# Mixers: transition products as alternating lines, and B's transition matrices copied without the identity

## The chip, the cores and the metric

The kernel runs on one core of a Trainium2 chip: one TensorE (PE), one VectorE (DVE), one ScalarE (ACT), one GpSimd (POOL), and SyncE (SP), which issues most of the DMAs. The metric is the device time of one execution in microseconds (us), and the time of a kernel is the median of its runs. A profiled execution lists every instruction with its start and length; its lines are called "rows" below.

## The reference

The reference is one decoder block on 16 meta tokens and 1024 tokens of width 1024: a gated FFN, a mixer, a second FFN, all with RMS norms. The mixer has two branches, which share one input projection: A, a chunked gated DeltaNet with 8 heads of 128, and B, an RWKV-7 time mixing with 16 heads of 64. The change is about branch B, whose core is a recurrence over the tokens:

```python
def _rwkv7_scan(r, w, k, v, a_vec, b_vec):
    def step(state, inp):
        r_t, w_t, k_t, v_t, a_t, b_t = inp
        sa = jnp.einsum('bhvk,bhk->bhv', state, a_t)
        state = state * w_t[:, :, None, :] + sa[..., None] * b_t[:, :, None, :] \
            + v_t[..., None] * k_t[:, :, None, :]
        return state, jnp.einsum('bhvk,bhk->bhv', state, r_t)
    ...
```

Over a chunk of 64 tokens this becomes one linear step for the state S of a head: S' = gam * (S + M S) + gam * N, where M (64 x 64, the chunk's *transition* without its identity) and N (the chunk's *value part*) hold no state and can be made ahead, and gam is the decay of the chunk.

## The kernel before

The kernel has three stages: the first FFN, the mixers (`middle`), the second FFN. Only the mixers matter here. The tokens are taken in two segments of 512 (the first with the 16 meta tokens, 528 columns), and each segment in 8 steps of 128 channels: one head of A and two heads of B. So there are 16 iterations, 0 to 7 and 8 to 15. An iteration projects its inputs (the `pp` products of line 314, against weights `w` that line 162 on ScalarE and line 163 on VectorE split into two parts), prepares operands, inverts triangular blocks, builds the transitions and runs the two chains. The actions are written in the order of the string `REGULAR`, and work of neighbouring iterations is written together. A scheduler then puts the instructions of all engines in one order by its own estimate of when each can run; each engine executes its own list strictly in that order. `issue_after` ties an instruction behind another on its engine.

The places that the change touches:

- `operands` makes, among much else, `grb` and `gra` (score products, emptied by VectorE into `LT`, `UA` and `attn`), `bkt` and `vp` (transposes, emptied by ScalarE), and at line 1636 16 products `vp<-LT,Vs`.
- `transitions` (line 1808) solves two sets of products `xp` (emptied by ScalarE into `xa` and into `xv`, which lies in the tile `at`), then makes 32 products `mp` and 32 products `np`. Half of mp is M, half goes to the read-out (`AR`); half of np is N (`vbk`), half goes to the output (`yb`).
- These are 64 x 64 products: each uses one quarter of the PE array, given by the half of the partitions that it reads (`src`) and the half that it writes (`dst`). `run` (line 1333) puts products with `src == dst` and with `src != dst` into two different PSUM banks, and chunk after chunk the products change between the two kinds. Without `line` the scheduler may take one bank's products first; with `line=()` `in_line` chains them in the order written, and with a list it also makes the first product wait for the instructions of that list.
- The pool `ch` has two PSUM banks, which xp, mp, np and all products of the chains take in turn; the next user of a bank waits until its last one has been read.
- Before, VectorE reads mp: four adds of 64 x 256 elements put M plus the identity into `g.mt` (line 1839), two adds go to `AR` (line 1842).
- `chains`: `chunk_a` runs the four steps of A (products `p`, `pq`), and behind two of its products it issues `chunk_b`, one step of B: a product `b` of `g.mt` with the state, then one VectorE instruction that gives the next state `SBs[:, i + 1]` (line 1915). `bm` and `am` are the start of the chains from the meta tokens, in the first segment only. At the end come the products `bq`.

Of the kernel before, what the change touches and what calls it, by code (L numbers as in the profile page):

```python
# [26 lines left out]
CB = 64  # L27
# [1295 lines left out]
def place(i, h):  # L1323

    return (i - h) % NCB // 2
# [7 lines left out]
def run(g, pool, name, *kinds, banks=(), line=None):  # L1333


    ps, out, used, todo = dict(enumerate(banks)), [], [0, 0], []
    for f in kinds:
        ds = [f(i, 0)[2] ^ f(i, 0)[3] for i in range(2)]
        one = ds[0] == ds[1]
        at = []  # L1340
        for d in ds:
            if d not in ps:
                ps[d] = pool.tile([P, 512], F32, name=name, tag=pool.name)
            at.append(used[d])
            used[d] += NCB // 2 * CB
        for i in range(NCB):
            e, c0 = ds[i & 1], at[0] + i * CB if one else at[i & 1] + i // 2 * CB
            for h in range(2):
                l, r, src, dst = f(i, h)
                assert src ^ dst == e  # L1350
                todo.append((ps[e][HS[dst], c0 : c0 + CB], l, r))
        if one:
            out.append([(ch3(ps[ds[0]][:, at[0] : at[0] + FULL], CB), slice(0, NCB))])
        else:
            out.append([(ch3(ps[d][:, c0 : c0 + NCB // 2 * CB], CB), cs) for d, c0, cs in zip(ds, at, EO)])
    products = [lambda x=x: g.nc.tensor.matmul(x[0], lhsT=x[1], rhs=x[2], start=True, stop=True) for x in todo]  # L1356
    if line is None:
        for p in products:
            p()
    else:  # L1360
        in_line(g, products, line)
    return out
# [171 lines left out]
def operands(g, q):  # L1534
# [98 lines left out]
        k = key(i, h)  # L1633
        return Vs[HS[k], i], LT[HS[k], i, 1 - (i & 1), CB:], k, h

    for ps, cs in run(g, g.mx, "vp", vr, banks=banks)[0]:
        nc.scalar.activation(ch3(yb, CB)[:, cs], ps, AF.Copy)
    if meta:
        btm = q.btm = st.tile([64, P], F32, name="btm", tag="btm", bufs=2)
# [168 lines left out]
def transitions(g, q):  # L1808

    nc, st = g.nc, g.st  # L1810
    Y = g.Y[q.it % 2]
    AR, LT, BKt, Vs, yb = q.AR, q.LT, q.BKt, q.Vs, ch3(q.yb, CB)
    vbk = q.vbk
    xa, xv, ar = st.tile([P, NCB, CB], F32, name="xa", tag="xa"), q.at, AR[:, NCB + 1 :]
    turned_bk, va, vb = by_key(g, q)
    vka = q.vka

    def solved(r, at=lambda i, h: i):
        def f(i, h):
            t = tok(i, h)  # L1820
            return Y[HS[t], i, HS[t]], r[HS[t], at(i, h)], t, t
        return f

    def by_tok(l, r):
        def f(i, h):
            t = tok(i, h)
            return l(HS[t], i), r(HS[t], i), t, h
        return f

    for ps, cs in run(g, g.ch, "xp", solved(q.at, lambda i, h: h * (NCB // 2) + place(i, h)))[0]:  # L1830
        nc.scalar.activation(xa[:, cs], ps, AF.Copy)
    for ps, cs in run(g, g.ch, "xp", solved(vka))[0]:
        nc.scalar.activation(xv[:, cs], ps, AF.Copy)
    bt = lambda r, i: turned_bk(HS.index(r), i, i & 1)
    br = lambda r, i: LT[r, i, i & 1, CB:]
    pm, pr = run(g, g.ch, "mp", by_tok(lambda r, i: xa[r, i], bt), by_tok(lambda r, i: xa[r, i], br))
    for ps, cs in pm:
        for hp in HS:
            nc.vector.tensor_tensor(g.mt[hp, cs, hp], ps[hp], g.C("ident")[hp, hp].unsqueeze(1).to_broadcast([CB, NCB // 2, CB]),
                                    op=ALU.add)  # L1840
    for ps, cs in pr:
        nc.vector.tensor_tensor(ar[:, cs], ps, ar[:, cs], op=ALU.add)
    pn, py = run(g, g.ch, "np", by_tok(bt, lambda r, i: xv[r, i]), by_tok(lambda r, i: xv[r, i], br))
    for ps, cs in pn:
        nc.vector.tensor_tensor(vbk[:, cs], ps, vbk[:, cs], op=ALU.add)
    nc.vector.tensor_tensor(vbk, vbk, q.gam.unsqueeze(2).to_broadcast([P, NCB, CB]), op=ALU.mult)
    for ps, cs in py:
        nc.vector.tensor_tensor(yb[:, cs], ps, yb[:, cs], op=ALU.add)


def chains(g, q):

    nc, st, c, j = g.nc, g.st, q.c, q.j
    meta = q.s == 0
    Y = g.Y[q.it % 2]
    S, SB = q.SA, q.SB
    Va, ktl, attn, egl = q.Va, q.ktl, q.attn, q.egl
    kqg = q.kq[:, :, q.off : q.off + FULL]
    hs = lambda h: slice(64 * h, 64 * h + 64)
    pt = lambda name: g.ch.tile([P, 512], F32, name=name, tag="ch")  # L1860
    if meta:
        ym, ltm, uvm = q.ym, q.ltm, g.uvm[q.it % 2]
        ps = pt("bm1")
        for h in range(2):
            nc.tensor.matmul(ps[32:48, hs(h)], lhsT=ltm[0:16, h, :], rhs=uvm[0:16, hs(h)], start=True, stop=True)
        rhm = st.tile([48, P], F32, name="rhm", tag="rhA", bufs=1)
        nc.vector.tensor_copy(rhm[32:48], ps[32:48, :P])
        ps = pt("bm2")
        for h in range(2):
            nc.tensor.matmul(ps[32:48, hs(h)], lhsT=ym[32:48, h, :], rhs=rhm[32:48, hs(h)], start=True, stop=True)  # L1870
        nc.scalar.activation(uvm[32:48, :], ps[32:48, :P], AF.Copy)
        ps = pt("bm3")
        for h in range(2):
            nc.tensor.matmul(ps[hs(h), :64], lhsT=q.btm[:, hs(h)], rhs=uvm[:, hs(h)], start=True, stop=True)
        for h in range(2):
            nc.vector.tensor_scalar(SB[hs(h)], ps[hs(h), :64], q.elm[hs(h), 16:17], None, op0=ALU.mult)
        ps = pt("am1")
        nc.tensor.matmul(ps[:16, :P], lhsT=ym[0:16, 2, :], rhs=q.vkm[:, 0, :], start=True, stop=True)
        vnm = st.tile([16, P], F32, name="vnm", tag="rhA", bufs=1)
        nc.scalar.activation(vnm, ps[:16, :P], AF.Identity, scale=c.tkm[:, j : j + 1])  # L1880
        ps = pt("am2")
        nc.tensor.matmul(ps[:, :P], lhsT=q.vkm[:, 1, :], rhs=vnm, start=True, stop=True)
        nc.vector.tensor_copy(S, ps[:, :P])
    oa = q.oa = kqg[:, 1, :]

    def chunk_a(i):
        csl = slice(i * CA, (i + 1) * CA)
        p1 = pt("p1")
        m = nc.tensor.matmul(p1[:, :P], lhsT=kqg[:, 0, csl], rhs=S, start=True, stop=True)  # L1889
        rh = st.tile([P, P], F32, name="rhA", tag="rhA", bufs=1)  # L1890
        nc.vector.tensor_tensor(rh, Va[:, i, :], p1[:, :P], op=ALU.subtract)
        with g.tc.issue_after(m.ins):
            chunk_b(2 * i)
        p2 = pt("p2")
        m = nc.tensor.matmul(p2[:, :P], lhsT=Y[:, NCB + i, :], rhs=rh, start=True, stop=True)
        with g.tc.issue_after(m.ins):
            chunk_b(2 * i + 1)
        vn = st.tile([P, P], F32, name="vn", tag="vn", bufs=2)
        nc.scalar.activation(vn, p2[:, :P], AF.Identity, scale=c.tk[:, i, j : j + 1])
        pq = pt("pq")  # L1900
        nc.tensor.matmul(pq[:, :CA], lhsT=S, rhs=kqg[:, 1, csl], start=True, stop=False)
        nc.tensor.matmul(pq[:, :CA], lhsT=vn, rhs=attn[:, i, :], start=False, stop=True)
        p3 = pt("p3")
        nc.tensor.matmul(p3[:, :P], lhsT=ktl[:, i, :], rhs=vn, start=True, stop=True)
        g.freed = [nc.vector.scalar_tensor_tensor(S, S, egl[:, i : i + 1], p3[:, :P], op0=ALU.mult, op1=ALU.add)]
        g.freed.append(nc.scalar.activation(oa[:, csl], pq[:, :CA], AF.Copy))


    SBs = st.tile([P, NCB + 1, CB], F32, name="SBs", tag="SBs")
    nc.gpsimd.tensor_copy(SBs[:, 0], SB)  # L1910

    def chunk_b(i):
        ps = pt("b1")
        nc.tensor.matmul(ps[:, :CB], lhsT=g.mt[:, i], rhs=SBs[:, i], start=True, stop=True)  # L1914
        nc.vector.scalar_tensor_tensor(SBs[:, i + 1], ps[:, :CB], q.gam[:, i : i + 1], q.vbk[:, i],
                                       op0=ALU.mult, op1=ALU.add)

    for i in range(NCA):
        chunk_a(i)
    ps = pt("bq")  # L1920
    todo = [lambda i=i, hp=hp: nc.tensor.matmul(ps[hp, i * CB : (i + 1) * CB], lhsT=SBs[hp, i], rhs=q.AR[hp, NCB + 1 + i],
                                                start=True, stop=True) for i in range(NCB) for hp in HS]
    if q.it + 1 < 2 * NJ:
        values(g, g.steps[q.it + 1], todo, g.freed)
    else:
        in_line(g, todo)
    nc.vector.tensor_tensor(q.yb, ps, q.yb, op=ALU.add)
    if meta:
        nc.sync.dma_start(g.sdr[j][:, :P], S)
        nc.sync.dma_start(g.sdr[j][:, P:], SBs[:, NCB])  # L1930
# [146 lines left out]
```

## Time and profile before

| | us |
|---|---|
| median of 3 runs | 2951.93 |
| lowest and highest run | 2947.85, 2956.73 |
| time of the profiled execution | 2947.13 |
| its span (first to last instruction) | 2945.0 |
| TensorE matmul rows of `mp`, busy, both halves | 21.2 + 16.9 |
| TensorE matmul rows of `np`, busy, both halves | 16.4 + 13.4 |
| VectorE `mt` adds (64) | 27.0 |
| VectorE `SBs` (128) | 35.9 |

A row of the groups reads: line, engine, operation, output<-inputs, partitions x elements, count | busy us, mean ns of one | idle us of the engine just before them, and what ended it. In the timeline a row has its start, its length, and in brackets the idle time before it with its releaser. A product in float32 is two records on TensorE, so 32 products show as x64 in the profile, while the orders that are shown with the change count products. Rows of matmuls overlap, since they are pipelined: what counts is the time from start to start.

### The profile page before, as it was taken

To read this page: it belongs to the slowest core of one execution; us is meant where nothing else is said; L and a number is where in the kernel's file an instruction comes from. 1 tells how busy PE (TensorE), PEld (TensorE's weight loads), DVE (VectorE), ACT (ScalarE), POOL (GpSimd) and SP (SyncE) were. 2 spreads that over 40 slices of the span, in tenths; PEclk is the share of its full clock that TensorE was granted. 3 is DMA by queue.
4 is the path that set the end of the run, shared out by engine and by line. 5 is a ranking of instruction groups with operands and counts; after the bars stand their busy time and mean duration, and the time that the engine had idled before them with its cause. 6 is when DMAs were issued, how large, how long until landed. Compare 5 with 4: busy or idle time off the path is not lost. (4 is left out here: it accounts for less than half of the span.)

```text
span 2945.0 us, 60773 instructions
## 1 busy us (share of the span) xinstructions
PE 2843.7 (97%) x24552; PEld 2465.6 (84%) x24552; DVE 2221.7 (75%) x4119; ACT 1445.9 (49%) x2511; POOL 523.0 (18%) x630
## 2 busy tenths in 40 slices
PE   8999999999989999999999999999999999999998
PEld 8999999999878887888777777777777788888787
DVE  8666668876678887788868888888867766667886
ACT  6322224336555656566565656656645422223443
POOL 0332332423010000000000110101101032222521
PEclk9999999999999999999999999999999999999999
DMA  5333236553232322333233332233455333323763
GB/s 214 126 109 109 95 111 218 183 191 125 69 76 75 87 68 70 80 83 93 84 95 75 82 82 73 79 87 88 108 137 187 128 108 107 104 100 129 240 219 111
DMA packets 287897, 339.17 MB, mean 115 GB/s; under 512 B 172704, under 2 KB 181024, under 8 KB 287616
## 3 DMA queue, kind: packets, MB, share of 16 engines
q1 hardware_dynamic: 283600, 326.10, 35.8%
q0 software_dynamic: 2000, 6.56, 0.6%
q8 instruction: 193, 3.16, 0.5%
q10 hardware_dynamic: 2016, 2.63, 0.3%
q14 instruction: 88, 0.72, 0.1%
HBM read 267.57 MB, written 73.41 MB: 116 GB/s over the span
## 5 line engine op out<-in xcount | busy, mean ns | idle before, releaser
L314 PE MATMUL pp<-uk,w 128*128 128x512 f32 (+2 forms) x4824 | 974.7, 347 | 15.0 <-ACT w L162 6.5
L314 PEld LDWEIGHTS pp<-uk,w 128*128 128x128 f32 x4824 | 742.6, 191 | 105.6 <-ACT w L162 6.8
L741 PE MATMUL pd<-form,w 128*128 128x256 f32 (+2 forms) x2904 | 437.0, 312 | 4.8 <-DVE w L163 4.8
L741 PEld LDWEIGHTS pd<-form,w 128*128 128x128 f32 x2904 | 402.4, 189 | 39.0 <-DVE w L163 6.8
L520 PE MATMUL pg<-bt,w 128*128 128x256 f32 (+2 forms) x2520 | 401.9, 317 | 2.9 <-DVE w L163 2.6
L520 PEld LDWEIGHTS pg<-bt,w 128*128 128x128 f32 x2520 | 360.2, 188 | 37.1 <-DVE w L163 3.8
L526 DVE TENSOR_TENSOR c<-c,pg 128x520 f32<-128x520 f32 (+1 forms) x280 | 189.5, 689 | 243.6 <-PE pg L520 220.1
L163 DVE TENSOR_TENSOR w<-wraw,w 128x1024 fp32r<-128x1024 f32 (+1 forms) x254 | 335.9, 1323 | 44.7 <-ACT w L162 42.5
L520 PE MATMUL pg<-b,w 128*128 128x256 f32 (+2 forms) x2160 | 348.1, 317 | 0.0
L162 ACT ACTIVATE w<-wraw 128x1024 fp32r<-128x1024 f32 (+1 forms) x254 | 267.2, 1052 | 149.8 <-PE pg L520 117.1
L520 PEld LDWEIGHTS pg<-b,w 128*128 128x128 f32 x2160 | 309.9, 188 | 28.2 <-DVE w L163 0.2
L162 ACT ACTIVATE w<-wrx 128x1024 fp32r<-128x1024 f32 (+1 forms) x64 | 58.4, 912 | 278.1 <-PE pg L520 243.0
L490 POOL TENSOR_TENSOR wrx<-wrx 128x512 f32<-128x512 f32 x38 | 52.5, 1382 | 612.5 <-DVE w22b L163 436.7
L163 DVE TENSOR_TENSOR form<-form 128x520 fp32r<-128x520 f32 (+1 forms) x152 | 142.0, 971 | 14.0 <-ACT form L162 13.8
L162 ACT ACTIVATE w<-wsum 128x768 fp32r<-128x768 f32 x96 | 75.7, 789 | 156.3 <-PE pd L741 123.1
L163 DVE TENSOR_TENSOR w<-wsum,w 128x768 fp32r<-128x768 f32 x96 | 118.4, 1238 | 36.3 <-ACT w L162 36.2
L241 POOL TENSOR_TENSOR wsum<-wsum,wraw 128x768 f32<-128x768 f32 (+1 forms) x48 | 97.8, 2051 | 202.8 <-DMA wraw<-in_wdn 190.0
L1705 DVE TENSOR_TENSOR Xb<-Xb,tb 115x126 f32<-115x126 f32 (+22 forms) x496 | 125.9, 254 | 9.7
L162 ACT ACTIVATE form<-form 128x520 fp32r<-128x520 f32 (+1 forms) x152 | 93.7, 631 | 78.0 <-DMA form<-frm 66.5
L1703 DVE TENSOR_TENSOR tb<-Ub,Xb 115x126 f32<-115x126 f32 (+22 forms) x496 | 124.7, 251 | 8.8
L1513 DVE SCALAR_TENSOR_TENSOR acc<-xr,pk,acc 128x528 f32<-128x528 f32 (+1 forms) x144 | 107.4, 757 | 6.7 <-ACT acc L1509 6.0
L314 PE MATMUL pwo<-uk,w 128*128 128x512 f32 x384 | 95.2, 398 | 0.9 <-DVE ho L1180 0.9
(445 smaller groups left out, 4360.3 us busy)
## 6 DMA issues: line engine op xcount, KB each, us to landing
wraw<-in_win SPq DMA_DIRECT2D x150, 512.0 KB
wraw<-in_wgu SPq DMA_DIRECT2D x44, 512.0 KB
wrx<-in_wgu SPq DMA_DIRECT2D x44, 512.0 KB
frm<-c SPq DMA_DIRECT2D x76, 260.0 KB
form<-frm SPq DMA_DIRECT2D x76, 260.0 KB
frm<-c SPq DMA_DIRECT2D x76, 256.0 KB
form<-frm SPq DMA_DIRECT2D x76, 256.0 KB
wraw<-in_wdn SPq DMA_DIRECT2D x34, 384.0 KB
```

The lines of the kernel that those rows point to most:

```text
L162: g.nc.scalar.activation(hi, src, AF.Copy)
L163: (eng or g.nc.vector).tensor_tensor(lo, src, hi.bitcast(F32), op=ALU.subtract)
L241: g.nc.gpsimd.tensor_tensor(s, x, y, op=ALU.add if r == 1 else ALU.subtract)
L314: g.last_product = g.nc.tensor.matmul(ps, lhsT=l, rhs=r, start=i == 0, stop=i == n - 1)
L490: sums.tensor_tensor(a22, a21, a22, op=ALU.add)
L520: nc.tensor.matmul(ps[:, c0 : c0 + cn], lhsT=l[:, x, k, :], rhs=r[:, k, y, c0 : c0 + cn], start=i == 0, stop=i == 3 * HK - 1)
L526: nc.vector.tensor_tensor(o, x, y, op=ALU.add)
L741: nc.tensor.matmul(pd[:, c0 : c0 + cn], lhsT=wd[:, u, k - k0, :], rhs=x[:, v, c0 : c0 + cn], start=k + i == 0, stop=k == HF - 1 and i == 2)
L1513: nc.vector.scalar_tensor_tensor(acc[:, :n], xr[:, tap : tap + n], V("convw", ct * 4 + tap), acc[:, :n], op0=ALU.mult, op1=ALU.add)
L1703: nc.vector.tensor_tensor(tv, U[:, i, i + 1 :].unsqueeze(2).to_broadcast([npt, nt, ncc]), X[:, i, 0:ncc].unsqueeze(1).to_broadcast([npt, n ...
L1705: nc.vector.tensor_tensor(X[:, i + 1 :, 0:ncc], X[:, i + 1 :, 0:ncc], tv, op=ALU.add)
```

## The change

Three things are changed. First, the `vp<-LT,Vs` products and the mp and np products become lines: even and odd chunks alternate between the two banks, and the first product of mp waits for both evictions of xp (`xa`, `xv`), the first of np for all six evictions of mp. Second, the four reads of M move from VectorE to ScalarE and leave the identity out: `g.mt` is M alone. Third, each chunk of B adds the missing gam * S to its value part with one more VectorE instruction (`rest`), and the state comes from the product and `rest`.

```diff
-    for ps, cs in run(g, g.mx, "vp", vr, banks=banks)[0]:
+    for ps, cs in run(g, g.mx, "vp", vr, banks=banks, line=())[0]:
...
+    freed = []
     for ps, cs in run(g, g.ch, "xp", solved(q.at, lambda i, h: h * (NCB // 2) + place(i, h)))[0]:
-        nc.scalar.activation(xa[:, cs], ps, AF.Copy)
+        freed.append(nc.scalar.activation(xa[:, cs], ps, AF.Copy))
     for ps, cs in run(g, g.ch, "xp", solved(vka))[0]:
-        nc.scalar.activation(xv[:, cs], ps, AF.Copy)
+        freed.append(nc.scalar.activation(xv[:, cs], ps, AF.Copy))
...
-    pm, pr = run(g, g.ch, "mp", by_tok(lambda r, i: xa[r, i], bt), by_tok(lambda r, i: xa[r, i], br))
+    pm, pr = run(g, g.ch, "mp", by_tok(lambda r, i: xa[r, i], bt), by_tok(lambda r, i: xa[r, i], br), line=freed)
+    freed = []
     for ps, cs in pm:
         for hp in HS:
-            nc.vector.tensor_tensor(g.mt[hp, cs, hp], ps[hp], g.C("ident")[hp, hp].unsqueeze(1).to_broadcast([CB, NCB // 2, CB]),
-                                    op=ALU.add)
+            freed.append(nc.scalar.activation(g.mt[hp, cs, hp], ps[hp], AF.Copy))
     for ps, cs in pr:
-        nc.vector.tensor_tensor(ar[:, cs], ps, ar[:, cs], op=ALU.add)
-    pn, py = run(g, g.ch, "np", by_tok(bt, lambda r, i: xv[r, i]), by_tok(lambda r, i: xv[r, i], br))
+        freed.append(nc.vector.tensor_tensor(ar[:, cs], ps, ar[:, cs], op=ALU.add))
+    pn, py = run(g, g.ch, "np", by_tok(bt, lambda r, i: xv[r, i]), by_tok(lambda r, i: xv[r, i], br), line=freed)
...
     def chunk_b(i):
         ps = pt("b1")
         nc.tensor.matmul(ps[:, :CB], lhsT=g.mt[:, i], rhs=SBs[:, i], start=True, stop=True)
-        nc.vector.scalar_tensor_tensor(SBs[:, i + 1], ps[:, :CB], q.gam[:, i : i + 1], q.vbk[:, i],
-                                       op0=ALU.mult, op1=ALU.add)
+        rest = q.vbk[:, i]
+        nc.vector.scalar_tensor_tensor(rest, SBs[:, i], q.gam[:, i : i + 1], rest, op0=ALU.mult, op1=ALU.add)
+        nc.vector.scalar_tensor_tensor(SBs[:, i + 1], ps[:, :CB], q.gam[:, i : i + 1], rest, op0=ALU.mult, op1=ALU.add)
```

The number of instructions on TensorE stays; the scheduler orders them anew from iteration 0 of the mixers on. Three places follow, in the order of the instructions on one engine, first before and then after the change (a row is a run of equal products or instructions).

TensorE, iteration 9, from the second xp to the first product of chain A (`p`), before:

```order
L1356 MATMUL xp<-vka,Y_7681 64x64 x16
L1356 MATMUL mp<-BKt,xa 64x64 x8
L1356 MATMUL mp<-LT,xa 64x64 x2
L1356 MATMUL mp<-BKt,xa 64x64 x8
L1356 MATMUL mp<-LT,xa 64x64 x14
L1551 MATMUL grb<-AR,BK 64x128 x11
L1590 MATMUL gra<-kq 128x256 x2
L1356 MATMUL np<-at,BKt 64x64 x16
L1356 MATMUL np<-LT,at 64x64 x16
L1590 MATMUL gra<-kq 128x256 x2
L314 MATMUL pp<-uk,w 128x512 x4
L1889 MATMUL p_20844<-SA,kq 128x128
```

and after:

```order
L1356 MATMUL xp<-vka,Y_7681 64x64 x16
L1551 MATMUL grb<-AR,BK 64x128 x7
L1356 MATMUL mp<-BKt,xa 64x64 x16
L1356 MATMUL mp<-LT,xa 64x64 x16
L1551 MATMUL grb<-AR,BK 64x128 x4
L1590 MATMUL gra<-kq 128x256 x4
L1356 MATMUL np<-at,BKt 64x64 x16
L1356 MATMUL np<-LT,at 64x64 x16
L314 MATMUL pp<-uk,w 128x512
L1388 MATMUL bkt<-ck,BK 128x64 x16
L314 MATMUL pp<-uk,w 128x512
L1890 MATMUL p_20916<-SA,kq 128x128
```

Seven grb products stand ahead of mp now and both pieces of gra ahead of np, while bkt has moved ahead of `p`, which has two pp ahead of it where there were four.

VectorE in the same iteration, from the weight split to the scaling of `vbk`, and then the start of the chains (`rhA` is A's first step there), before:

```order
L163 TENSOR_TENSOR w<-wraw,w 128x1024
L1839 TENSOR_TENSOR mt<-mp,ck 64x4x64 x4
L1842 TENSOR_TENSOR AR<-mp,AR 128x4x64 x2
L1554 TENSOR_TENSOR LT<-grb,ck 128x4x128 x2
L1594 SCALAR_TENSOR_TENSOR UA<-gra,tk,E 128x128 x2
L1596 TENSOR_TENSOR attn<-gra,E 128x256
L1845 TENSOR_TENSOR vbk<-np,vbk 128x4x64 x2
L1848 TENSOR_TENSOR yb<-np,yb 128x4x64
L1846 TENSOR_TENSOR vbk<-vbk,gam 128x512
```

```order
L1891 TENSOR_TENSOR rhA<-Va,p_20844 128x128
L1915 SCALAR_TENSOR_TENSOR SBs<-b_20848,gam,vbk 128x64
L1915 SCALAR_TENSOR_TENSOR SBs<-b_20853,gam,vbk 128x64
L1647 TENSOR_TENSOR ktl<-ktp,kts 128x512
L1653 TENSOR_TENSOR kq<-kq,gp 128x2x512
```

and after, up to the `yb` add, and the start of the chains:

```order
L1554 TENSOR_TENSOR LT<-grb,ck 128x4x128
L1843 TENSOR_TENSOR AR<-mp,AR 128x4x64 x2
L1554 TENSOR_TENSOR LT<-grb,ck 128x4x128
L1594 SCALAR_TENSOR_TENSOR UA<-gra,tk,E 128x128 x2
L1596 TENSOR_TENSOR attn<-gra,E 128x256
L1594 SCALAR_TENSOR_TENSOR UA<-gra,tk,E 128x128 x2
L1596 TENSOR_TENSOR attn<-gra,E 128x256
L1846 TENSOR_TENSOR vbk<-np,vbk 128x4x64 x2
L1849 TENSOR_TENSOR yb<-np,yb 128x4x64
```

```order
L1892 TENSOR_TENSOR rhA<-Va,p_20916 128x128
L1917 SCALAR_TENSOR_TENSOR vbk<-SBs,gam,vbk 128x64
L1647 TENSOR_TENSOR ktl<-ktp,kts 128x512
L1653 TENSOR_TENSOR kq<-kq,gp 128x2x512
L1918 SCALAR_TENSOR_TENSOR SBs<-b_20920,gam,vbk 128x64
L1917 SCALAR_TENSOR_TENSOR vbk<-SBs,gam,vbk 128x64
L1918 SCALAR_TENSOR_TENSOR SBs<-b_20926,gam,vbk 128x64
```

The `mt` adds are gone, both pairs of UA and attn now precede `vbk` and `yb`, and `rest` (written as `vbk<-SBs,gam,vbk`) follows each state; `ktl` and `kq`, which stood behind two states, stand ahead of the first.

VectorE in iteration 3, before:

```order
L1945 TENSOR_TENSOR zg<-pp,zg 128x512
L1839 TENSOR_TENSOR mt<-mp,ck 64x4x64 x4
L1842 TENSOR_TENSOR AR<-mp,AR 128x4x64 x2
L1554 TENSOR_TENSOR LT<-grb,ck 128x4x128 x2
L163 TENSOR_TENSOR w<-wraw,w 128x1024
L1845 TENSOR_TENSOR vbk<-np,vbk 128x4x64 x2
```

and after:

```order
L1947 TENSOR_TENSOR zg<-pp,zg 128x512
L163 TENSOR_TENSOR w<-wraw,w 128x1024
L1843 TENSOR_TENSOR AR<-mp,AR 128x4x64
L1554 TENSOR_TENSOR LT<-grb,ck 128x4x128
L1843 TENSOR_TENSOR AR<-mp,AR 128x4x64
L1554 TENSOR_TENSOR LT<-grb,ck 128x4x128
L1846 TENSOR_TENSOR vbk<-np,vbk 128x4x64 x2
```

The weight split has moved from behind LT to ahead of the first `AR` add, and one LT stands between the two adds; on ScalarE the first half of that split stands directly ahead of the four copies.

## The prediction

> **What bounds the kernel now.** I read the page first, then the busy time in stretches of 85 us, the groups by line, and the timeline of two iterations.
>
> ```profile
> span 2945.0 us, 60773 instructions
> PE 2843.7 (97%) x24552; PEld 2465.6 (84%) x24552; DVE 2221.7 (75%) x4119; ACT 1445.9 (49%) x2511; POOL 523.0 (18%) x630
> ```
>
> ```profile
> core 0: us, PE busy (x) PEld busy (x) DVE busy (x) ACT busy (x) POOL busy (x), PEclk, DMA share, GB/s
> ...
> 1105.00:1190.00 85.00, 81.28 (x998) 69.46 (x998) 66.28 (x167) 51.88 (x107) 3.83 (x17) 1.00 0.25 72
> ...
> 1785.00:1870.00 85.00, 82.58 (x879) 65.21 (x874) 71.10 (x166) 53.18 (x100) 8.69 (x18) 1.00 0.31 84
> ```
>
> TensorE is busy for 81 to 83 of 85 us in the stage of the mixers, VectorE for 66 to 71, ScalarE for about 52. So a saving counts only if TensorE's own sequence gets shorter: fewer or faster products, or a wait of TensorE that goes. All that the change touches lies in this stage (16 iterations, from 850 to 2245 us).
>
> ```profile
> L1356 PE MATMUL np<-at,BKt 64*64 64x64 f32 x512 | 16.4, 232 | 10.8 <-DVE AR L1842 10.8
> L1839 DVE TENSOR_TENSOR mt<-mp,ck 64x256 f32<-64x256 f32 x64 | 27.0, 422 | 20.2 <-PE mp L1356 19.6
> L1842 DVE TENSOR_TENSOR AR<-mp,AR 128x256 f32<-128x256 f32 x32 | 12.1, 420 | 0.2
> L1915 DVE SCALAR_TENSOR_TENSOR SBs<-b,gam,vbk 128x64 f32<-128x64 f32 x128 | 35.9, 280 | 23.7 <-PE b L1914 22.8
> ```
>
> The wait that the change aims at is the first row's: the np products stand 10.8 us in all until VectorE has emptied the bank that they take, behind four `mt` adds and an `AR` add, one after another.
>
> **Speed of the products.** Iteration 9 on TensorE, from the timeline; the last number is the time from start to end of the row, the brackets an idle time before it:
>
> ```profile
> 1705.02 1.15 PE L1356 MATMUL xp<-vka,Y 64*64 64x64 f32 x32 [0.27 <-DVE Y L1769]
> 1706.00 0.63 PE L1356 MATMUL mp<-BKt,xa 64*64 64x64 f32 x16
> 1706.46 0.28 PE L1356 MATMUL mp<-LT,xa 64*64 64x64 f32 x4
> 1706.87 0.62 PE L1356 MATMUL mp<-BKt,xa 64*64 64x64 f32 x14
> ...
> 1707.85 1.04 PE L1551 MATMUL grb<-AR,BK 64*64 64x128 f32 x22
> 1708.82 1.13 PE L1590 MATMUL gra<-kq 128*128 128x256 f32 x4
> 1710.29 0.88 PE L1356 MATMUL np<-at,BKt 64*64 64x64 f32 x27 [0.34 <-DVE AR L1842]
> ...
> 1711.70 1.13 PE L1590 MATMUL gra<-kq 128*128 128x256 f32 x4
> 1712.48 1.28 PE L314 MATMUL pp<-uk,w 128*128 128x512 f32 x4
> 1713.66 0.46 PE L1889 MATMUL p<-SA,kq 128*128 128x128 f32 x2
> ...
> 1718.66 0.96 PE L1356 MATMUL vp<-LT,Vs 64*64 64x64 f32 x32
> ...
> 1731.41 0.27 PE L1921 MATMUL bq<-AR,SBs 64*64 64x64 f32 x2
> ...
> 1771.76 0.69 PE L1356 MATMUL vp<-Vs,BKt 64*64 64x64 f32 x32
> 1772.38 2.11 PE L314 MATMUL pp<-uk,w 128*128 128x512 f32 x8
> ```
>
> A product is two records here. The 64 records of mp take 1706.00 to 1707.85, 1.85 us, among them a standstill before 1706.87: one bank's even products run, then the odd ones wait for the second bank. The 64 of np take 1710.29 to 1711.70, 1.41 us. The row at 1771.76 is a line that already alternates: its 32 take 0.62 us until the next work, and start over about 0.48 (0.69 less the 0.22 of one record), so 64 take 0.62 + 0.48 = 1.10. With the same pace mp saves **0.75**, np **0.31**, and the vp products at 1718.66 (0.96 against 0.69) **0.27**: 1.33 us an iteration. I take the full pace, because the order of even and odd products in the new lines is that of the row at 1771.76; the other end is no gain.
>
> **Evictions.** What empties the banks, on VectorE and then ScalarE:
>
> ```profile
> 1707.98 1.73 DVE L1839 TENSOR_TENSOR mt<-mp,ck 64x256 f32<-64x256 f32 x4 [1.89 <-PE mp L1356]
> 1709.72 0.76 DVE L1842 TENSOR_TENSOR AR<-mp,AR 128x256 f32<-128x256 f32 x2
> 1710.39 1.28 DVE L1554 TENSOR_TENSOR LT<-grb,ck 128x512 f32<-128x512 f32 x2
> 1711.59 0.60 DVE L1594 SCALAR_TENSOR_TENSOR UA<-gra,tk,E 128x128 f32<-128x128 f32 x2
> ...
> 1712.44 0.75 DVE L1845 TENSOR_TENSOR vbk<-np,vbk 128x256 f32<-128x256 f32 x2
> 1713.10 0.42 DVE L1848 TENSOR_TENSOR yb<-np,yb 128x256 f32<-128x256 f32 x1
> ...
> 1719.36 1.22 DVE L1653 TENSOR_TENSOR kq<-kq,gp 128x1024 f32<-128x1024 f32 x1
> ```
>
> ```profile
> 1706.22 0.60 ACT L1833 ACTIVATE at<-xp 128x512 f32<-128x512 f32 x1 [0.82 <-PE xp L1356]
> 1716.66 1.09 ACT L1621 ACTIVATE BKt<-bkt 128x512 f32<-128x512 f32 x2 [9.85 <-PE bkt L1388]
> 1718.22 0.66 ACT L1629 ACTIVATE at<-vp 128x256 f32<-128x256 f32 x2 [0.22 <-PE vp L1388]
> ```
>
> ScalarE stands idle for 9.85 us just there, so the copies find it free in iteration 9. Two copies of this width take 0.66, so each further one about 0.28 and four about 1.2 us (on 64 partitions, between nothing and this). The program makes each `AR` add wait for the copies of its own bank; I take them one behind the other, so the last add ends 1.2 + 0.1 + 0.42 = 1.7 us after the products, against 2.5 before (1.73 + 0.76). The Trainium skill (PSUM — Partial Sum Buffer, section "PSUM bank collisions raise a hardware error") says that two engines must not be in the same bank on the same partitions at once, reads included. By that the 1.7 stands; if copies and adds ran side by side it would be 1.3, and the sum some 1 us lower. No run here shows it yet.
>
> **The step through iteration 9**, by the order that is shown with the change. `grb` runs 22 records in 0.97 (1707.85 to 1708.82), so the seven products that now stand before mp take 0.62: 1706.62. The mp line needs both banks, and the second is free as before (the copy at 1706.22 ends at 1706.82): it starts at 1706.87 after 0.25 of waiting and ends at 1707.97. Then 0.35 of grb, and both pieces of gra (1.13 + 0.78 = 1.91): 1710.23. The banks are empty at 1708.1 + 1.7 = 1709.8, so np starts without a wait and ends at 1711.33, 0.37 earlier than before with all of gra behind it. Next come two pp (0.23 each) and bkt (0.65): TensorE asks for `p` at 1712.44. But `p` takes the bank that np's `yb` add empties, and VectorE now has both UA and attn pairs (0.85 each, 1711.59 to 1712.44) ahead of it: 1709.8 + 0.65 (LT) + 1.7 + 0.66 + 0.42 = 1713.2, so `p` starts at 1713.3, 0.85 late and only 0.36 earlier than 1713.66. Behind it `kq` (1.22) now stands ahead of the first SBs; the second `b` product waits some 0.35 for it. From `p` to `bq` it was 17.75 us (1713.66 to 1731.41); now bkt is done (-0.65), vp is faster (-0.27), one more pp lies inside (+0.23), and there is the 0.35: 17.4. So `bq` comes at 1730.7, 0.7 earlier, with one pp (0.23) left for later: **0.5 us** for each of iterations 8 to 14, of 1.33 + 0.34 that products and the old np wait could give.
>
> **The first eight iterations** differ; from iteration 3, on TensorE, VectorE and ScalarE:
>
> ```profile
> 1127.37 0.68 PE L1356 MATMUL mp<-BKt,xa 64*64 64x64 f32 x16 [0.35 <-ACT xa L1831]
> ...
> 1129.35 1.04 PE L1551 MATMUL grb<-AR,BK 64*64 64x128 f32 x28
> ...
> 1131.79 0.86 PE L1356 MATMUL np<-at,BKt 64*64 64x64 f32 x26 [0.97 <-DVE AR L1842]
> ...
> 1135.45 0.38 PE L1865 MATMUL bm<-uvm,ltm 16*16 16x64 f32 x4 [1.13 <-DVE yb L1848]
> ```
>
> ```profile
> 1133.09 1.22 DVE L163 TENSOR_TENSOR w<-wraw,w 128x1024 fp32r<-128x1024 f32 x1
> ...
> 1128.74 1.04 ACT L162 ACTIVATE w<-wraw 128x1024 fp32r<-128x1024 f32 x1
> ```
>
> Here mp takes 1.98 (to 1129.35) and now waits for its second bank, until 1128.4, and ends at 1129.5. ScalarE holds a weight split (1128.74, 1.04) ahead of the copies, and VectorE the other half (1.22) ahead of the first `AR` add, which was behind LT before: 1129.8 + 1.22 + 0.38 + 0.65 + 0.38, so np starts at 1132.5, 0.7 later than before, although it waits for less. It ends at 1133.6; `vbk` and `yb` follow at once, no split between, and `bm` starts at 1135.0, 0.45 earlier, with three more pp done (0.69): **1.1 us** for iterations 3 to 6. In 1 and 2 a split goes ahead of the copy `xa` instead; there I take 0.9, between 0 and the 2 of the products and the waits. In 0, 7 and 15 other work lies between, and I take about half of the 1.33, 0.7.
>
> **What is added to the chain.** 128 VectorE instructions of 128x64 with no operand in PSUM; the nearest row is SBs, 280 ns, so 128 x 0.28 = 36 us of VectorE at most, and 27.0 go with `mt`: at most +9 us on an engine that has 14 of 85 us free. Each needs only the state of the chunk before and runs while TensorE makes `b`, so it hides; if it stood in the way each time it would add up to 36 us. I take nothing. ScalarE gets 64 x about 0.28 to 0.39 = 18 to 25 us, beside 33 idle of 85.
>
> **Sum:** 7 x 0.5 + 4 x 1.1 + 2 x 0.9 + 3 x 0.7 = 11.8, so 12 us less: 2947.13 becomes 2935 for the profiled execution. It lies 4.8 under the median of the runs, 2951.93; from that, **2940 us**.
>
> **Rivals.**
> - The waits go as well as the products: `p` finds its bank sooner than I worked out. For it: the instructions that delay it are short and my steps add up their row lengths. Products 16 x about 1.25 (1.33 less what vp gains in iteration 9) = 20, np's waits 10.8: 31 us, 2921.
> - All is swallowed at the banks. For it: in iteration 9 three quarters of the gain already end at `p`; with 0.5 us more on VectorE nothing is left, and likewise if the pace of the line is not reached. Against: bm's and np's 1.1 and 0.97 us of waiting in the first segment. Between -5 and +5: 2950. The Trainium skill (TensorEngine Tiling (Array Packing), section "Performance Considerations", "PSUM Bottleneck") says that packing makes TensorE faster, not the emptying of PSUM, which may then be the limit. The trace agrees as far as it goes: mp in 1.85, its bank emptying in 2.5.
> - Slower: one late copy holds all 32 products. np now asks for all six evictions, where its first half asked for one bank's. If a weight split's two halves (1.04 + 1.22 = 2.3) stand in front of the copies in 15 iterations, not in some, that is 34 - 12 = +22: 2974. It decides from 0.8 us of new waiting an iteration. For it: iterations 3 to 6; against: in iteration 9 the split is over before (ScalarE idle 9.85).
>
> **How the numbers follow.** The forecast (6 to 18 us less) 0.52, the full gain 0.14, swallowed 0.24, slower 0.10. A measurement of this kernel tells about 0.3% (9 us) from no change. Faster by more: 0.14 and some four fifths of the forecast, 0.56; within: 0.34; slower: 0.10. The range goes from the full gain to the upper end of the swallowed case, 2920 to 2957, and leaves out the slower one; the forecast's own is 2934 to 2946.
>
> **What would show it.** In the changed profile: mp's and np's 64 records in 1.1 us; np's wait smaller or gone in iteration 9, and a wait of `p` on `yb` of about 0.85; in iteration 3 np still waiting, bm less; 128 new instructions of 0.2 to 0.28 us with no wait of SBs behind them. Wrong would be: mp still at 1.8, TensorE waiting on `mt`, or a longer time from `p` to `bq`.

## The result, and the profile after

The changed kernel is slower: 2966.33 us, the median of 5 runs (2964.66 to 2970.34), against 2951.98 (5 runs, 2947.85 to 2956.73). The ratio is 1.0053, with a 95% interval from 1.0041 to 1.0065: 14 us more, where 12 us less were predicted. The profiled execution of the changed kernel took 2970.34 us, 4 us over its median, and the one of before lay 5 us under its own, so the two profiles stand 23 us apart. Of the experiments below, one execution of e1 that took 3421.2 us at a granted clock of 0.75 is left out of its ratio and its means.

The page of the changed kernel, its first part:

```profile
span 2968.6 us, 60945 instructions
...
PE 2850.5 (96%) x24552; PEld 2461.4 (83%) x24552; DVE 2221.2 (75%) x4183; ACT 1473.2 (50%) x2575; POOL 521.8 (18%) x630
```

TensorE executes as many instructions as before and is busy 7 us longer, although the products were to become faster. The groups of the changed kernel that answer to those shown of before:

```profile
L314 PE MATMUL pp<-uk,w 128*128 128x512 f32 (+2 forms) x4824 | 988.8, 350 | 19.0 <-DVE w L163 10.0 <-ACT w L162 6.2 <-DVE uk L163 1.3
...
L1917 DVE SCALAR_TENSOR_TENSOR vbk<-SBs,gam,vbk 128x64 f32<-128x64 f32 x128 | 36.1, 282 | 2.0
L1918 DVE SCALAR_TENSOR_TENSOR SBs<-b,gam,vbk 128x64 f32<-128x64 f32 x128 | 36.0, 281 | 18.0 <-PE b L1915 16.3
...
L1841 ACT ACTIVATE mt<-mp 64x256 f32<-64x256 f32 x64 | 24.1, 377 | 14.4 <-PE mp L1356 13.6
...
L1356 PE MATMUL np<-at,BKt 64*64 64x64 f32 x512 | 12.3, 230 | 1.9 <-DVE AR L1843 1.9
```

np's wait, the aim of the change, fell from 10.8 to 1.9 us. But the weight products `pp`, which the change does not touch, now wait 10.0 us for VectorE's half of the weight split. And np's wait did not go, it moved. The waits of TensorE in the mixers (who waited for whom: us in total, times, longest) name where TensorE waits now:

```profile
PE mp L1356 <- ACT at L1834: 7.5, 14, 1.0
PE grb L1551 <- DVE LT L1554: 5.9, 5, 2.3
PE bkt L1388 <- DVE attn L1596: 5.5, 7, 0.8
...
PE np L1356 <- DVE AR L1843: 1.9, 2, 1.2
```

Between 850 and 2245 us the waits of mp, grb, np, bkt, `bm` and `p` add up to 20.3 us before the change and to 25.0 after it. So what the step gains comes from the pace of the products.

Where the time came from is read by stretches. The borders are starts of rows in the timelines; the brackets hold what a halved TensorE clock can have cost at most, half of the time at half speed (e1 and e6 are experiments below):

| us, in the profiled execution | before | after | e1 | e6 |
|---|---|---|---|---|
| start to the first `vp<-LT,Vs` of iteration 0 | 788.4 (1.9) | 788.1 (1.8) | 792.1 (3.8) | 791.6 (3.5) |
| to mp of iteration 1 | 153.0 (8.3) | 159.0 (15.3) | 157.4 (13.3) | 154.2 (10.2) |
| to mp of iteration 7 | 599.7 (3.4) | 597.7 (8.5) | 595.3 (5.1) | 594.7 (5.1) |
| to mp of iteration 9 | 164.9 (3.4) | 167.8 (6.8) | 167.7 (6.8) | 168.3 (6.8) |
| to mp of iteration 14 | 424.1 (0) | 440.2 (6.8) | 420.8 (0) | 421.2 (0) |
| to the end | 814.8 (3.3) | 815.8 (4.9) | 811.3 (3.2) | 811.7 (3.4) |

Up to this first border TensorE, VectorE, ScalarE and GpSimd execute the same instructions in the same order in all eleven kernels, and still the stretch takes from 787.8 to 796.5 us in their profiles: a few us in one row of one execution show nothing by themselves. Iterations 9 to 13 are five repetitions of one step. 16 of the 24 us arise in them, and they were even before (84.8 us each) and the prediction's best understood place. Iteration 9 of the changed kernel on TensorE, from the timeline, with ScalarE's copies and the `AR` adds between:

```profile
1712.58 0.69 PE L1356 MATMUL mp<-BKt,xa 64*64 64x64 f32 x32 [0.21 <-ACT at L1834]
...
1713.09 0.65 PE L1356 MATMUL mp<-LT,xa 64*64 64x64 f32 x32
...
1713.77 1.56 ACT L1841 ACTIVATE mt<-mp 64x256 f32<-64x256 f32 x4 [1.25 <-PE mp L1356]
...
1713.89 1.99 PE L1590 MATMUL gra<-kq 128*128 128x256 f32 x8
...
1715.37 0.42 DVE L1843 TENSOR_TENSOR AR<-mp,AR 128x256 f32<-128x256 f32 x1 [0.35 <-ACT mt L1841]
...
1715.85 0.69 PE L1356 MATMUL np<-at,BKt 64*64 64x64 f32 x32
...
1716.36 0.65 PE L1356 MATMUL np<-LT,at 64*64 64x64 f32 x32
...
1718.23 0.71 PE L1388 MATMUL bkt<-ck,BK 64*128 64x64 f32 x16 [0.79 <-DVE attn L1596]
...
1719.23 0.46 PE L1890 MATMUL p<-SA,kq 128*128 128x128 f32 x2
...
1736.33 0.27 PE L1923 MATMUL bq<-AR,SBs 64*64 64x64 f32 x2
```

The 64 records of mp take 1712.58 to 1713.74, 1.16 us, those of np 1715.85 to 1717.01, also 1.16, and np does not wait. From mp to `bq` it is 23.75 us, against 25.4 before (of which some 0.6 are seven `grb` products that now stand ahead of mp). Up to here the iteration is as predicted. What follows `bq`, from the same timeline:

```profile
1739.56 0.63 ACT L1305 ACTIVATE AR<-yb 128x512 f32<-128x512 f32 x1 [0.88 <-DVE yb L1929]
...
1742.71 4.76 PE L314 MATMUL pp<-uk,w 128*128 128x512 f32 x20
...
1745.58 1.05 ACT L162 ACTIVATE w<-wraw 128x1024 fp32r<-128x1024 f32 x1
...
1747.64 1.22 DVE L1422 TENSOR_TENSOR_SCAN Ls<-ck,sw 128x512 f32<-128x512 f32 x1
...
1748.15 0.73 PE L314 MATMUL pp<-uk,w 128*128 128x512 f32 x2 [0.68 <-ACT w L162]
...
1748.93 1.22 DVE L163 TENSOR_TENSOR w<-wraw,w 128x1024 fp32r<-128x1024 f32 x1
...
1750.21 6.87 PE L314 MATMUL pp<-uk,w 128*128 128x512 f32 x22 [1.33 <-DVE w L163]
```

And the same place before the change:

```profile
1732.02 1.05 ACT L162 ACTIVATE w<-wraw 128x1024 fp32r<-128x1024 f32 x1
...
1733.26 1.22 DVE L163 TENSOR_TENSOR w<-wraw,w 128x1024 fp32r<-128x1024 f32 x1
...
1735.60 0.63 ACT L1305 ACTIVATE AR<-yb 128x512 f32<-128x512 f32 x1
...
1738.34 9.02 PE L314 MATMUL pp<-uk,w 128*128 128x512 f32 x39
```

Before, ScalarE split the next weight ahead of the epilogue of branch B (which begins with `AR<-yb`), and 39 weight products ran through. Now the split stands 6 us behind the epilogue's start, VectorE's half of it stands behind the scan `Ls`, and TensorE, with no other weight left, waits 0.68 + 1.33 = 2.0 us. The 22 products behind the wait start slowly, too. TensorE's clock is granted in windows of 3.41 us (the last section works this out); one at 0.50 is called slow here. The windows view of the changed kernel around the wait (length, then busy us and instructions of each engine, granted clock, DMA share, GB/s):

```profile
1743.69:1747.10 3.41, 3.41 (x17) 2.74 (x15) 3.27 (x10) 3.41 (x7) 0.00 (x0) 1.00 0.00 0
1747.10:1750.52 3.42, 1.41 (x5) 0.60 (x4) 3.42 (x7) 2.62 (x6) 0.42 (x1) 1.00 0.00 0
1750.52:1753.93 3.41, 3.41 (x9) 2.65 (x8) 3.28 (x10) 0.49 (x3) 1.16 (x1) 0.50 0.71 228
1753.93:1757.34 3.41, 3.41 (x34) 2.59 (x36) 2.44 (x11) 0.23 (x1) 0.00 (x0) 1.00 0.32 118
```

In the window that holds the wait TensorE is busy for 1.41 us; in the next one its clock is 0.50, 9 records run where 17 ran, and 1.7 us are lost. The first three of the five iterations by their own windows, mp to mp:

```profile
1712.58:1800.87 88.29, 83.44 (x868) 64.83 (x868) 71.58 (x170) 54.56 (x102) 8.12 (x18) 0.98 0.30 81
1800.87:1889.23 88.36, 83.48 (x869) 64.83 (x869) 71.71 (x170) 54.55 (x102) 8.12 (x18) 0.98 0.30 80
1889.23:1976.04 86.81, 81.88 (x869) 63.64 (x869) 71.56 (x170) 54.55 (x102) 9.23 (x18) 1.00 0.32 82
```

Where no slow window follows the wait (the third row) an iteration takes 86.8 us, in the other four 88.2 to 88.6.

### The profile page after: what moved, and what is told of

It reads as the page before. It is cut to its first block, busy times and chain, and to the rows that moved or that the text cites. A ratio compares the mean times of both kernels' runs of the same rounds, so it can differ in the third digit from the quotient of the medians.

```text
span 2968.6 us, 60945 instructions
## 1 busy us (share of the span) xinstructions
PE 2850.5 (96%) x24552; PEld 2461.4 (83%) x24552; DVE 2221.2 (75%) x4183; ACT 1473.2 (50%) x2575; POOL 521.8 (18%) x630
## 4 chain that ended last, share of the span: by engine, by line
PE 68%; DVE 16%; ACT 8%; DMA 4%; issue 3%; POOL 1%; SPq 1%; DVEq 0%; POOLq 0%; ACTq 0%
PE pg L520 25%; PE pp L314 19%; PE pd L741 8%; DVE w L163 2%; PE pwo L314 2%; PE pg L544 2%; DVE Xb L1705 1%; DVE tb L1703 1%; DMA form<-frm 1%; DVE form L163 1%; ACT w L162 1%; PE cs L1292 1%; PE b L1915 1%; PE p L1890 1%; PE iv L1743 1%
## 5 line engine op out<-in xcount | busy, mean ns | idle before, releaser
L314 PE MATMUL pp<-uk,w 128*128 128x512 f32 (+2 forms) x4824 | 988.8, 350 | 19.0 <-DVE w L163 10.0
L314 PEld LDWEIGHTS pp<-uk,w 128*128 128x128 f32 x4824 | 753.6, 193 | 118.9 <-DVE w L163 13.5
```

What stands on the lines that cost most here:

```text
L314: g.last_product = g.nc.tensor.matmul(ps, lhsT=l, rhs=r, start=i == 0, stop=i == n - 1)
```

## The experiments

The theories. **A**: the scheduler's new place for the weight split costs the time. **B**: the new work on ScalarE and VectorE does. **C**: the lines do, since they wait for both banks. **G**, a part of A: the wait costs more than its length, by the clock. The experiments were timed in five rounds beside the kernel before, whose median lay between 2951.3 and 2952.1 us in each series. The last column is the time that the clock withheld, span times one less the granted clock, as the mean of all executions of a kernel; it is the most that the clock can have cost. (Granted clocks are on record to 0.001, 3 us in an execution, and before has 24.5 to 25.6 us by series, so a difference of 1 or 2 us says little.)

| kernel | median us | ratio to before, 95% interval | us per iteration, 9 to 13 | withheld by the clock, us |
|---|---|---|---|---|
| before | 2951.98 | | 84.8 | 25.0 |
| after | 2966.33 | 1.0053 [1.0041, 1.0065] | 88.0 | 37.4 |
| e1_pinned | 2946.99 | 0.9986 [0.9972, 0.9999] | 84.2 | 30.8 |
| e2_lines | 2947.80 | 0.9991 [0.9983, 1.0000] | 85.3 | 24.3 |
| e3_copies | 2952.34 | 1.0002 [0.9993, 1.0011] | 85.1 | 25.3 |
| e4_norest | 2966.77 | 1.0056 [1.0041, 1.0070] | 87.8 | 35.1 |
| e5_fill | 2959.32 | 1.0029 [1.0018, 1.0039] | 86.9 | 31.3 |
| e6_start | 2945.81 | 0.9980 [0.9971, 0.9988] | 84.2 | 28.9 |
| e7_pin_novp | 2948.34 | 0.9989 [0.9979, 0.9999] | 84.2 | 25.4 |
| e8_start78 | 2956.73 | 1.0020 [1.0009, 1.0030] | 84.2 | 33.7 |
| e9_startfill | 2946.41 | 0.9979 [0.9969, 0.9989] | 84.3 | 25.7 |

**e1_pinned: the split back in its place.** In `finish`, for iterations 9 to 14; `fetchw` writes a weight's fetch and both halves of its split, here ahead of the epilogue (`colsum_rsqrt`), and `g.splits` collects ScalarE's halves:

```diff
...
-    colsum_rsqrt(g, "bd", yb, sq, rg, FULL, 1.0 / 64, V("gneps"), pool="ch")
+    with ExitStack() as behind:
+        if NJ < q.it < 2 * NJ - 1:
+            fetchw(g)
+            behind.enter_context(g.tc.issue_after(g.splits[-1].ins))
+        colsum_rsqrt(g, "bd", yb, sq, rg, FULL, 1.0 / 64, V("gneps"), pool="ch")
```

> The changed kernel with one thing moved: in iterations 9 to 14 the weight split that the scheduler had put behind the epilogue of chain B goes back ahead of it on ScalarE, as before the change. Theory A (the order of the weight splits costs the time: 2.0 us of waiting of the weight products in each of these iterations, and in most of them one half-speed window of the clock, 1.7 us): the wait of pp on w is gone there, the period of these iterations falls from about 88.3 to about 84.8 us, the clock stays at 1.00 in most of them, and the time is 15 to 21 us under the changed kernel, 2945 to 2952. Theory B (the new VectorE and ScalarE work of the change costs it): the period stays over 87 us and the time at 2960 or more.

Its timeline at the same place (its line numbers are 3 higher), and two rows of its windows, mp to mp:

```profile
1738.60 1.06 ACT L162 ACTIVATE w<-wraw 128x1024 fp32r<-128x1024 f32 x1
...
1740.07 0.63 ACT L1308 ACTIVATE AR<-yb 128x512 f32<-128x512 f32 x1
...
1744.55 7.89 PE L317 MATMUL pp<-uk,w 128*128 128x512 f32 x34
```

```profile
1712.60:1796.77 84.17, 81.09 (x868) 63.89 (x868) 70.96 (x170) 54.56 (x102) 8.04 (x18) 1.00 0.32 84
1796.77:1880.94 84.17, 81.06 (x868) 63.88 (x868) 71.06 (x170) 54.56 (x102) 8.03 (x18) 1.00 0.31 85
```

The split is ahead again, no product waits for it, the clock stays at 1.00, and the five iterations take 420.8 us in place of 440.2. The ratio falls by 0.67%, some 20 us. Theory A holds, B falls: all the work that the change adds is still there. The change without the late split is 4.7 us faster than before. The means over all executions say the same in two parts: beside before in its own series e1 has 5.2 us more withheld by the clock (30.8 against 25.6) and is 9 us shorter in the rest.

**e2_lines and e3_copies: one half of the change each.** e2 keeps VectorE's four `mt` adds and the old `chunk_b`; e3 drops the three `line` arguments:

```diff
# e2, against the changed kernel
-            freed.append(nc.scalar.activation(g.mt[hp, cs, hp], ps[hp], AF.Copy))
+            freed.append(nc.vector.tensor_tensor(g.mt[hp, cs, hp], ps[hp], ..., op=ALU.add))
-        rest = q.vbk[:, i]
...
# e3, against the changed kernel; likewise for np and vp
-    pm, pr = run(g, g.ch, "mp", ..., line=freed)
+    pm, pr = run(g, g.ch, "mp", ...)
```

> The lines alone (mp, np and the second vp), with VectorE's mt adds with the identity and chunk B's one instruction as before the change. Theory A (the scheduler keeps the split ahead of the epilogue here): no wait of pp on w in iterations 9 to 14, a period of 84 to 84.8 us there, and a time 5 to 12 us under before, 2940 to 2947. Rival C (a line that waits for both banks costs more than its pace gives): as slow as the changed kernel, 2960 or more.

> The copies alone: ScalarE copies the transitions without the identity and each chunk adds the term to its value part, but no product is put into a line. Theory A (the split stays ahead of the epilogue here too): within 5 us of before, 2947 to 2957, with a period of 84.5 to 85.3 us in iterations 9 to 14. Theory B (the copies and the 128 new instructions cost the time): 2960 or more.

Neither is slow: as the cause of the 14 us C falls, and B once more. In both the split stays ahead of the epilogue. Neither speeds up iterations 9 to 13 by itself, though: 85.3 and 85.1 us against 84.8. In e2, np waits 12.4 us in all for VectorE's reads of mp, in e3 9.8. Only the two together, with the split in its place, give 84.2. e2's period was expected half a microsecond lower, and its time came out 0.8 us above the expected range.

**e4_norest: without the new VectorE work.** `chunk_b` is the old one, on the changed kernel.

> The changed kernel without the 128 new instructions of chain B; it leaves out the identity's term (gam times the state) from every step of chain B. The split stands behind the epilogue in iterations 9 to 14 as in the changed kernel. Theory A: these instructions are hidden; pp waits for w about 2 us an iteration as in the changed kernel, and the time is within 5 us of it, 2961 to 2971. Theory B (VectorE's 36 us of new work is the cost): the period of iterations 9 to 14 falls to 86 us or less and the time to 2955 or less.

The time is that of the changed kernel, and the split is late as there (33.1 us after mp's start in iteration 9, behind the epilogue at 27.1). The 36 us of VectorE are hidden, as the prediction took them.

**e5_fill: useless products in the wait.** Ahead of the weight products that wait, in iterations 9 to 13:

```diff
+    if fill:
+        with g.tc.issue_after(g.last_product.ins):
+            for _ in range(fill):
+                g.nc.tensor.matmul(ps, lhsT=g.sums["ones"], rhs=rhs(0)[0], start=True, stop=True)
...
+    k = shifted(g, c, 40 + j, 8 + j, "kB", fill=8 if it > NJ + 2 else 0)
```

> The changed kernel, with the weight split where the scheduler put it, and eight useless products (ones times the first tile, overwritten by the real ones) on TensorE directly ahead of the weight products that wait, in iterations 9 to 13. Theory G (what the wait costs beyond its own 2.0 us is the clock: a window of 3.41 us in which TensorE idles over about 0.4 of the time is followed by one at half speed, 1.7 us lost): the eight products fill about 1.7 us of the wait, no half-speed window follows it, the period falls from about 88.3 to about 86.8 us although 40 products were added, and the time is about 7 us under the changed kernel, 2957 to 2962. Rival H (the clock has nothing to do with this wait): the half-speed windows stay and the time is 2964 or more; if the products cost their own time, 2970 or more.

The timeline of iteration 9 (`pp<-uk,onesr` are the useless ones), and the window of that iteration:

```profile
1741.25 2.00 PE L314 MATMUL pp<-uk,onesr 128*128 128x512 f32 x8
...
1744.64 5.30 PE L318 MATMUL pp<-uk,w 128*128 128x512 f32 x22 [0.46 <-DVE w L163]
```

```profile
1706.99:1793.88 86.89, 83.48 (x877) 65.30 (x877) 71.55 (x170) 54.60 (x102) 9.03 (x18) 1.00 0.31 82
```

With 40 products more the kernel is 7 us faster. The weight comes no sooner (ScalarE's split starts 33.0 us after mp's start in both, and the products that need VectorE's half start 37.6 us after it), the period is that of the changed kernel's one undisturbed iteration (86.8), but none of the five is followed by a slow window, and the 22 products take 5.30 us in place of 6.87. Over all executions the clock withholds 31.3 us, in the changed kernel 37.4. Theory G holds.

**e6_start, e7_pin_novp, e8_start78: what the lines do elsewhere,** all on top of e1_pinned. With the lines iteration 0 had become longer (157.4 us against 153.0):

```diff
# e6: mp and np likewise; e8 has "q.it not in (0, NJ - 1, NJ)"; e7 has no line for vp at all
-    for ps, cs in run(g, g.mx, "vp", vr, banks=banks, line=())[0]:
+    for ps, cs in run(g, g.mx, "vp", vr, banks=banks, line=() if q.it else None)[0]:
```

> e1_pinned with no lines in iteration 0 alone (mp, np and the second vp there in the order of before). Theory S (with the lines the scheduler spreads the work ahead of iteration 0 so that two waits fall into neighbouring clock windows and two to four windows run at half speed, where before had one): from the first vp to iteration 1's mp it takes 152 to 154 us in place of 157.4, and the time is 3 to 5 us under e1_pinned, 2941 to 2944. Rival L (those windows are luck of the clock's grid): no difference from e1_pinned, 2945 to 2949.

> e1_pinned without the line of the second vp. If the prediction's 0.27 us an iteration for it counts in full, the period of iterations 9 to 13 grows from 84.2 to about 84.5 us and the time by 4 us to about 2951; if it is swallowed by a wait behind it, period and time stay, 2945 to 2949.

> e6_start with no lines in iterations 7 and 8 either. In e1_pinned these two take 167.7 us from iteration 7's mp to iteration 9's, against 164.9 before the change. Theory S: about 165 us there and 2 to 3 us under e6_start. Rival L: no difference from e6_start.

In its profile e6 shortens the stretch to 154.2 us as expected, and loses 3.1 us less there to the clock. The time falls by 1.2 us, less than expected, and the intervals of e1 and e6 overlap: the gain is not certain in the time. The profiles of the other kernels narrow the place down: the stretch takes 156.9 to 159.0 us, 12.4 to 15.3 of them withheld, in the four kernels with both the copies and vp's line in iteration 0 (after, e1, e4, e5), and 152.8 to 155.4 with 8.3 to 10.2 in the seven others. e7, which leaves out vp's line alone, is one of these. All that is withheld there lies ahead of iteration 0's mp. e6 is faster than both the kernel before and the changed one.

In e7 the period stays 84.2: the line of vp gains nothing in these iterations. Over the whole kernel two differences from e1 nearly cancel, each taken beside before in its own series: 4.3 us less withheld by the clock and 4.6 us more in the rest. What made them was not taken apart.

e8 went against its theory: 173.2 us in place of 168.3 for iterations 7 and 8, 601.8 in place of 594.7 before them, 12 us more in all. (This execution, 2963.7 us, is e8's slowest, 7 us over its median.) Nine windows at half speed lie between 1450 and 1640 us there, against six in e6. What made them was not taken apart, so what the lines do in iterations 7 and 8 stays open.

**e9_startfill: useless products ahead of three more tiles of weight products,** on top of e6 with the edit of e5. The three times in its expectation count from 11.3 us before the profile's zero: in the profile the waits are at 825, 843 and 1605 us.

> e6_start with useless products (overwritten by the real ones) ahead of three tiles of weight products that wait 2.0, 3.4 and 2.8 us for their weight in its profile (at 836, 854 and 1616 us): 16 of half width, 12 and 10. Theory G: the waits stay, the half-speed windows after them (one at 843 us in e6_start, and by the clock's grid in some executions one after each of the others) go: 1.7 to 5 us under e6_start, 2941 to 2944. Rival: the windows there come from other waits, or the products cost their own time: 2945.8 or up to 5 us more.

No difference from e6 in the time (0.9979 against 0.9980). From its timeline (products only):

```profile
838.12 0.96 PE L321 MATMUL pp<-uk,w 128*128 128x512 f32 x3 [0.66 <-DVE w L163]
...
847.09 1.07 PE L1753 MATMUL iv<-Xc,LT 32*32 32x32 f32 x32 [2.37 <-DMA Xc<-scX]
...
1594.18 1.77 PE L317 MATMUL pp<-uk,onesr 128*128 128x512 f32 x7
...
1606.83 5.02 PE L321 MATMUL pp<-uk,w 128*128 128x512 f32 x11 [2.77 <-DVE w L163]
```

The first wait is gone, the second is 0.66 us in place of 3.40, and the slow windows that e6 has behind them, at 826 and 843 us, are gone. But TensorE then waits 2.37 us at 847 us for a DMA, where e6 waits 0.93, and a stretch of two slow windows came there. The third set of useless products ends 7 us before the wait that it was meant for begins, with other products between; that wait is as long as in e6 and falls among slow windows in both. So the third wait was not put to the test. Beside before in its own series, e6 has 4.4 us more withheld and is 10.8 us shorter in the rest, e9 0.9 and 6.9. The expectation was wrong: what the clock gave back, something else took.

## Why the prediction failed, point by point

- **Speed of the products: right.** 1.10 us was predicted to the start of the next product; by that measure mp takes 0.98 to 1.09 in all 16 iterations, and 1.16 from its first start to its last end. np takes 1.16 to 1.25 to its last end in 14 iterations, and 2.0 and 2.3 in iterations 1 and 6.
- **Evictions: a little too short.** A copy takes 377 ns in mean, and four in iteration 9 take 1.56 us, not 1.2, and the last `AR` add ends 2.05 us after the products (1715.79 against 1713.74), not 1.7. It cost nothing, since gra keeps TensorE busy until np.
- **The step through iteration 9: right to 0.1 us, as far as it went, in part by luck.** From mp to `bq` 23.8 us were predicted (1706.87 to 1730.7) and 23.75 measured. Its two parts miss by more and cancel: mp to `p` 6.43 predicted and 6.65 measured, `p` to `bq` 17.4 and 17.1. The 0.27 for vp in it is worth nothing to the period (e7). The wait of 0.85 us that was set at `p` came as 0.79 at bkt, one place earlier, which the same `attn` holds up.
- **The step that failed: "So `bq` comes at 1730.7, 0.7 earlier, with one pp (0.23) left for later: 0.5 us for each".** The walk ended at `bq` and took the rest of the iteration as unchanged. Behind `bq` the order had changed too, on ScalarE: the next weight's split had moved behind the epilogue. e1 shows that this cost some 20 us. With the split in place the five iterations gain 3.3 us, 0.66 each, where 0.5 was predicted.
- **A term that was missing: the clock.** The sum priced each wait by its length. In the third row of the mp-to-mp windows above the wait costs 86.81 - 84.17 = 2.6 us, and in the four others 1.4 to 1.7 more for a slow window. e5 shows that these two parts can be had apart.
- **Iterations 0 and 7: wrong in sign, as far as single executions show.** "I take about half of the 1.33, 0.7": the stretches of iteration 0 and of 7 and 8 became 6.0 and 2.9 us longer, and 4.4 and 2.8 in e1. In iteration 0 the clock can account for all of it (5.0 us more in e1's bracket), and e6 and e7 point to the lines as what brings it; for 7 and 8 the cause stays open (e8). e1 gains 4.7 us and not 12: without what the clock withheld it is 9 us shorter than before.
- **Iterations 1 to 6: mis-sized.** Predicted 6.2 us less (1.8 + 4.4); measured 2.0 less in the changed kernel, with 5.1 us more lost to the clock than before, and 4.4 less in e1. There iterations 1 and 2 gain 1.0 each, where 0.9 was predicted, and 3 to 6 from -0.1 to 1.3, where 1.1 was. In iteration 3 `bm` comes 6.5 us after mp, as the walk has it (6.6), so what is missing lies behind the walk's end here too; which work takes it stays open.
- **`rest` and the load of ScalarE: right.** 36.1 us hidden (e4), copies 24.1 us, predicted 18 to 25.
- **The rivals.** The slower one named a weight split, but put it ahead of the copies of mp, where it would hold the np products; it set 0.8 us of new waiting an iteration as the point from which it decides. The wait was 2.0 us, and it stood where the walk did not look.

The split moves only when both halves of the change are there (e2, e3), and it moves without `rest` (e4). Why the scheduler does so was not tried.

## What to carry to other kernels

When a scheduler orders the program, a local edit can move an instruction that it does not touch: compare the whole period of every engine's list, and above all the place of the loads and splits that feed the busiest engine, not only the surroundings of the edit. Walk the step to the same point one period later, not to the last instruction that the edit names. Price a new wait on TensorE by what it does to the clock as well.

## What the runs showed of the hardware

TensorE's clock is halved in whole windows of 3.41 us on a fixed grid: in each of the eleven profiles all slow windows begin within 4 ns of one grid. What makes one slow is the window before it. Of 115 full-speed windows in which TensorE was idle for 0.4 or more of the time (1.4 us; worked out from its rows), 92 were followed by a slow one, among them all 63 with 0.55 or more (1.9 us); of 9153 with less than 0.4, 7. (The first 13 to 15 us of each execution, ahead of the trace's first clock entry, and the last windows at its end are left out.) The Trainium skill (TensorE: Matmul & The Clock Gate, section "What's actually happening") states such free-running windows of 3413 ns and two states, full and half; the trace agrees. It puts the fall to half speed after an idle window. Here a wait of 2.0 us is enough when most of it lies in one window, and 1.4 us often is.

So a wait is dearer than it looks, by up to 1.7 us, depending on where the grid lies in an execution, and two waits of a microsecond close to each other can cost as much as one of two: in 24 of the 115 windows no single idle time reached 1.2 us, and 22 of them were followed by a slow one. In its profiled execution the changed kernel lost up to 44 us to half speed, the kernel before 20 (the brackets of the table of stretches); over all executions it is 37 and 25, so a part of what parts the two profiles is the execution that was profiled. That useless products made a kernel faster by 7 us (e5) follows from it; that the time stayed in e9, although the clock withheld less, shows that such a gain cannot be counted on where other waits lie close by.
